# Low parts of float32r weight blocks: an accumulating DMA onto the negated high part in place of a VectorE subtraction

## The chip, the cores and the metric

The kernel runs on one core of a Trainium2 chip. The metric is device time in microseconds (us) of one execution; the lower, the better.

## The reference

A trunk of two decoder layers over 512 tokens of width 1024, all in float32. Each layer adds three things to the residual stream `x`, each of them after an RMSNorm:

```python
x = x + 0.5 * swiglu(rmsnorm(x, g1), w_gate1, w_up1, w_down1)   # 1024 -> 2816 -> 1024
p = rmsnorm(x, gm) @ w_in                                       # 1024 -> 3328, three mixers share it
x = x + concat(gmlp(p[:512]), shortconv(p[512:1280]), retention(p[1280:])) @ w_out
x = x + 0.5 * swiglu(rmsnorm(x, g2), w_gate2, w_up2, w_down2)
```

A final RMSNorm ends it. Nearly all of the arithmetic is in the products with the weights. A weight matrix is used once, so each of its 512 KB blocks is loaded from HBM once (in the kernel before) and used by 24 matmuls.

## The kernel before

**Products in parts.** TensorE takes float32r operands, which keep fewer bits than float32. So each operand `a` is split in a high part, `a` rounded to float32r, and a low part, what the rounding left over. A product is then three matmuls: high by high, high by low, low by high. `mm3` (L97) issues them as L99, L100 and L101. Activations are split once (`xh`, `xl`, and the two halves of `h`), weights block by block in `load` (L88): a DMA from SyncE brings 128x1024 float32 into `raw` (L92), ScalarE copies it with rounding into `whi` (L93), and VectorE subtracts `whi` from `raw` into `wlo` (L94). Some blocks hold 128x896. `load` is called 336 times; the first two blocks of the program are made in `start` (L185), in halves, with subtractions of their own (L210), which the change leaves alone.

**Buffers.** `raw` has 4 buffers, `whi` and `wlo` have 3 each (L83 to L85). A new block's `whi` and `wlo` can be written when the block three places before it has been used by its last matmul. Each engine works through its instructions in the order in which they were put in its queue; the tile framework orders them when the program is built, and puts the semaphore waits in.

**Stages.** In `gate_up` (L149) the weights are the stationary operand: block after block of 24 matmuls, first gate and then up of each of 22 feature tiles; behind each pair `finish` makes silu(gate) x up and splits it (VectorE L157, L160, L105, ScalarE L158, L104). In `ffn` (L217) the down product goes through pieces of 8, 7 and 7 blocks of 128 columns, 24, 21 and 21 matmuls (weights stationary, so the low weight part is first used by L101, the third matmul). `mixer` (L291) projects with 26 blocks; for values and gates (`project_tokens`) and in the last down product (`last_ffn`, L233) the tokens are the stationary operand and the low weight part is used by L100, the second matmul. Between them stand the small matmuls of retention and gMLP and the layer norms (`layernorm`, L495), whose reciprocal root is a GpSimd power (L510). GpSimd otherwise makes 1/rms in `norm_columns` (L134), masks a table (L302), and makes the final norm's factor (L285).

**End of the program.** The last three blocks of the last down product are all loaded ahead (L269), one into each buffer, and then used for one 128-token chunk and half of the features after the other, so that the final norm and the stores of a chunk run under the matmuls of the next.

Of the kernel before, what the change touches and what calls it, by code (L numbers as in the profile page):

```python
# [9 lines left out]
F32 = mybir.dt.float32  # L10
F32R = mybir.dt.float32r
AF = mybir.ActivationFunctionType
ALU = mybir.AluOpType
AX = mybir.AxisListType

P = 128
D = 1024
T = 512
DEPTH = 2
FF = 2816  # L20
KT = D // P
# [8 lines left out]

# Columns of the packed per-feature parameters.
G1, GM, G2 = 0, 8, 16
GV, GN, CW = 24, 26, 30
PER = 36
NPAR = DEPTH * PER

# Columns of the packed position constants.
C_COS, C_SIN, C_DEC, C_XI, C_ZETA = 0, 512, 1024, 1536, 2048
# [4 lines left out]
def trunk(ctx, tc, xt, w_gu1, w_dn1, w_in, w_out, w_gu2, w_dn2, w_last, par, con, wst, bst, gain, out):  # L43
    nc = tc.nc
# [19 lines left out]

# [1 line left out]
    x = [xpool.tile([P, T], F32, tag=f"x{k}", name=f"x{k}") for k in range(KT)]  # L66
    xh = [xpool.tile([P, T], F32R, tag=f"xh{k}", name=f"xh{k}") for k in range(KT)]
    xl = [xpool.tile([P, T], F32R, tag=f"xl{k}", name=f"xl{k}") for k in range(KT)]
    pcol = cpool.tile([P, NPAR], F32, name="pcol")
# [18 lines left out]
    def load(src):  # L88
        """One block of weights as two float32r parts whose sum it is."""
        n = src.shape[-1]  # L90
        raw, hi, lo = weight_tiles()
        nc.sync.dma_start(raw[:, :n], src)  # L92
        nc.scalar.copy(hi[:, :n], raw[:, :n])  # L93
        nc.vector.tensor_tensor(lo[:, :n], raw[:, :n], hi.bitcast(F32)[:, :n], ALU.subtract)  # L94
        return hi, lo

    def mm3(ps, ah, al, bh, bl, first, last):  # L97
        """ps += a.T @ b from their parts."""
        nc.tensor.matmul(ps, lhsT=ah, rhs=bh, start=first, stop=False)  # L99
        nc.tensor.matmul(ps, lhsT=ah, rhs=bl, start=False, stop=False)  # L100
        nc.tensor.matmul(ps, lhsT=al, rhs=bh, start=False, stop=last)  # L101
# [5 lines left out]
    state = {}  # L107
    warm_ps = bank("warm")

    def norm_part(k, gcol):  # L110
        """x[k] times its gain in two parts."""
        g = pcol[:, gcol + k : gcol + k + 1]
        nc.scalar.activation(xh[k], x[k], AF.Copy, scale=g)  # L113
        nc.vector.scalar_tensor_tensor(xl[k], x[k], g, xh[k].bitcast(F32), ALU.mult, ALU.subtract)  # L114
# [10 lines left out]
    def norm_columns():  # L125
        """1 / rms of each token, as columns [token, chunk]."""
        acc = state["acc"]
        ps = bank(uniq("pss"))
        for n in range(NCH):
            nc.tensor.matmul(ps[:, n : n + 1], lhsT=acc[:, n * P : (n + 1) * P], rhs=ones[:, 0:1], start=True, stop=True)  # L130
        ms = spool.tile([P, NCH], F32, tag="ms", name=uniq("ms"))
        nc.vector.tensor_scalar(ms, ps[:, :NCH], 1.0 / D, EPS, ALU.mult, ALU.add)
        rc = spool.tile([P, NCH], F32, tag="rc", name=uniq("rc"))
        nc.gpsimd.tensor_tensor(rc, ms, mhalf[:, :NCH], ALU.pow)  # L134
        state["rc"] = rc

    def norm_rows():
        """1 / rms of each token along the free axis, on every partition."""
        rc = state["rc"]
        pr = bank(uniq("psr"))  # L140
        dg = spool.tile([P, NCH, P], F32, tag="dg", name=uniq("dg"), bufs=1)
        for n in range(NCH):
            nc.vector.tensor_scalar(dg[:, n, :], ident, rc[:, n : n + 1], None, ALU.mult)
            nc.tensor.matmul(pr[:, n * P : (n + 1) * P], lhsT=ones, rhs=dg[:, n, :], start=True, stop=True)
        rr = spool.tile([P, T], F32, tag="rr", name=uniq("rr"))
        nc.scalar.copy(rr, pr)
        state["rr"] = rr

    def gate_up(l, w_gu, first=False):  # L149
        """h = silu(rms gate) * up, features on partitions."""  # L150
        hs = []
# [13 lines left out]
        for f in range(FT):  # L165
            ps = []
            if first and f == 0:
                ps = start(w_gu[l, 0, 0], w_gu[l, 1, 0])
            else:
                for j in range(2):  # L170
                    hi, lo = load(w_gu[l, j, f])
# [13 lines left out]
    def start(gate, up):  # L185
        """The first two blocks, with the splits of x between the first products."""
        for k in range(12):
            warm = warm_ps[:, (k % 4) * P : (k % 4 + 1) * P]
            nc.tensor.matmul(warm, lhsT=ones, rhs=ones, start=True, stop=True)
        ps = [bank(uniq("pgu")) for _ in range(2)]  # L190
        w = [weight_tiles() for _ in range(2)]
# [41 lines left out]
    def last_ffn(l, w_gu):  # L233
        """The last feed-forward, its second product and the final norm with tokens on partitions."""
        state.pop("rr", None)
        xtok = {}
        for f, hs in enumerate(gate_up(l, w_gu)):
            if f not in (4, 6):
                continue
            s = f // 6  # L240
# [50 lines left out]
    def mixer(l, after):  # L291
# [15 lines left out]
        def project(block, name):  # L307
            """One 128-feature block of the projection, features on partitions."""
            hi, lo = load(w_in[l, block])
            p = bank(uniq(name))  # L310
            for k in range(KT):
                c = slice(k * P, (k + 1) * P)
                mm3(p, hi[:, c], lo[:, c], xh[k], xl[k], k == 0, k == KT - 1)
            return p

        def project_tokens(block, name):
            """512 features of the projection (four blocks), tokens on partitions."""
            ps = [bank(uniq(name)) for _ in range(NCH)]
            for j in range(4):
                hi, lo = load(w_in[l, block + j])  # L320
                for n in range(NCH):
                    t = slice(n * P, (n + 1) * P)
                    for k in (2 * j, 2 * j + 1):
                        c = slice((k % 2) * T, (k % 2 + 1) * T)
                        mm3(ps[n], xh[k][:, t], xl[k][:, t], hi[:, c], lo[:, c], k == 0, k == KT - 1)
            return ps

        # Retention: rotated queries and keys.
        qk = [big(uniq("q")) for _ in range(2)] + [big(uniq("k")) for _ in range(2)]
        head = lambda w, h: qk[2 * w + h // 2][:, (h % 2) * T : (h % 2 + 1) * T]  # noqa: E731  # L330
        ahead = [project(0, "pqk")]
# [4 lines left out]
        for w in range(2):  # L336
            for h in range(HEADS):
# [10 lines left out]
                nc.vector.tensor_tensor(o, o, s, ALU.add)  # L348
        # Values, tokens on partitions.
        vt = [big(uniq("vt")) for _ in range(2)]  # L350
        tok = lambda tiles, n: tiles[n // 2][:, (n % 2) * T : (n % 2 + 1) * T]  # noqa: E731
        for n, p in enumerate(project_tokens(8, "pv")):
            nc.scalar.activation(tok(vt, n), p, AF.Copy, scale=rc[:, n : n + 1])
        # Queries for the state, keys with their decay to the chunk's end.
        qx = [big(uniq("qx")) for _ in range(2)]
# [18 lines left out]
        ys = [None] * KT  # L374
        # gMLP values, tokens on partitions.
        av = big(uniq("av"))
        hi, lo = load(w_in[l, 16])
        hi2, lo2 = load(w_in[l, 17])
        for n in range(NCH):
# [6 lines left out]
            nc.scalar.activation(av[:, n * 256 : (n + 1) * 256], p[:, :256], AF.Gelu_apprx_tanh, scale=rc[:, n : n + 1])  # L386
        # States ahead of chunks 1..3.
        st = [big(uniq("st")) for _ in range(2)]
# [19 lines left out]
        layernorm(av, av, NCH * AG, AH)  # L408
        # Gates.
        sg = [big(uniq("sg")) for _ in range(2)]  # L410
# [3 lines left out]
        for n in range(NCH):  # L414
# [11 lines left out]
            nc.vector.tensor_tensor(tok(yn, n), tok(yn, n), tok(sg, n), ALU.mult)  # L426
        # Short convolution.
        def conv(j):
# [5 lines left out]
            nc.vector.tensor_tensor(z[:, :T], z[:, :T], rr, ALU.mult)  # L434
            w = lambda i: pcol[:, base + CW + 2 * i + j : base + CW + 2 * i + j + 1]  # noqa: E731
            o = z[:, T:]
# [26 lines left out]
        conv(1)  # L463
        # Retention's outputs, features on partitions.
        for h in range(HEADS):
# [7 lines left out]
            ys[4 + h] = y  # L473
        # gMLP gates.
        for j in range(2):
# [19 lines left out]
    def layernorm(dst, src, groups, width):  # L495
        """(src - mean) / sqrt(var + eps) over groups of the free axis."""
        s3 = src.rearrange("p (g d) -> p g d", g=groups)
# [33 lines left out]
def _constants(np):  # L531
    """What depends on positions alone: rotary tables, decays."""
    half = P // 2
# [9 lines left out]
    scale = P**-0.5  # L543
# [8 lines left out]
def _layout(np, inp):  # L552
    """The inputs, each weight block as one contiguous run per partition."""
    f = lambda n: np.asarray(inp[n])  # noqa: E731
    arrays = {"xt": f("x").reshape(T, KT, P).transpose(2, 1, 0)}
# [7 lines left out]
    w = f("w_in")  # L563
    cols = lambda a, n: w[:, :, a : a + n]  # noqa: E731
    wide = lambda a, n, b: cols(a, n).reshape(DEPTH, b, KT // b, P, n).transpose(0, 1, 3, 2, 4).reshape(DEPTH, b, P, 1024)  # noqa: E731
    tall = lambda a, b: cols(a, b * P).reshape(DEPTH, KT, P, b, P).transpose(0, 3, 2, 1, 4).reshape(DEPTH, b, P, 1024)  # noqa: E731
    c0 = 1280
# [3 lines left out]
    arrays["w_out"] = f("w_out").reshape(DEPTH, KT, P, KT, P).transpose(0, 3, 2, 1, 4).reshape(DEPTH, KT, P, 1024)  # L571
    per = lambda a, n: a.reshape(n, P).T  # noqa: E731
    par = []
# [30 lines left out]
```

## Time and profile before

| | |
|---|---|
| time, median of 2 runs | 1877.43 us (1877.14 to 1877.72) |
| span of the profiled execution, first to last instruction | 1875.7 us |
| TensorE busy | 1865.6 us, 99% |
| VectorE busy | 839.3 us, 45% |
| ScalarE busy | 567.2 us, 30% |
| GpSimd busy | 27.4 us, 1% |
| read from HBM | 178.56 MB |

The profile is of one execution; its span leaves out what lies before the first and after the last instruction, here 1.7 us against the median of the timed runs. Engines are PE (TensorE), PEld (its weight loads), DVE (VectorE), ACT (ScalarE), POOL (GpSimd), SP (SyncE). Matmuls are pipelined: a row gives each 0.39 us, but one starts every 0.23 us, so it is starts that are compared. An issue of a DMA isn't counted as busy time.

### The profile page before, as it was taken

The page shows a single profiled execution, that of the slowest core. Times are in us where ns is not written, and L with a number is a line of the kernel's source. Part 1 is how long each engine was busy: PE and PEld are TensorE (multiplying, and loading weights), DVE is VectorE, ACT ScalarE, POOL GpSimd, SP SyncE. Part 2 cuts the span into 40 slices and gives each one's busy share as a digit, 9 for nine tenths or more (in the row PEclk, how much of TensorE's full clock was granted, in tenths as well). Part 3 has the DMA queues.
Part 4 walks back from the last instruction along what each step waited for, and adds up shares of the span by engine and source line. Part 5 has one row for each costly group of instructions (what it writes and reads, how often), then busy time and mean ns, then how long its engine had stood idle before and what let it go on. Part 6 is the DMA issues. An engine that isn't in the chain of part 4 may idle for free.

```text
span 1875.7 us, 20497 instructions
## 1 busy us (share of the span) xinstructions
PE 1865.6 (99%) x8560; PEld 1554.4 (83%) x8560; DVE 839.3 (45%) x1052; ACT 567.2 (30%) x713; POOL 27.4 (1%) x34
## 2 busy tenths in 40 slices
PE   9999999999999999999999999999999999999998
PEld 7888888888888888888888888888888888888886
DVE  5344334474664434433443444344647543444224
ACT  5223222223343322322232232222132433323212
POOL 0000000000000000000000000000000000000000
PEclk9999999999999999999999999999999999999999
DMA  5232333322222232233323223333322222332321
GB/s 203 102 97 94 99 93 93 114 94 75 84 90 97 95 101 91 99 93 95 106 90 102 91 100 96 94 93 108 102 79 79 91 92 89 100 100 92 113 94 64
DMA packets 52860, 181.98 MB, mean 97 GB/s; under 512 B 6048, under 2 KB 6560, under 8 KB 52640
## 3 DMA queue, kind: packets, MB, share of 16 engines
q1 hardware_dynamic: 52624, 180.64, 29.8%
q8 instruction: 67, 1.10, 0.2%
q14 instruction: 25, 0.20, 0.0%
q10 hardware_dynamic: 144, 0.04, 0.0%
HBM read 178.56 MB, written 2.10 MB: 96 GB/s over the span
## 4 chain that ended last, share of the span: by engine, by line
PE 98%; issue 0%; ACT 0%; DMA 0%; DVE 0%; SPq 0%; POOL 0%; POOLq 0%; ACTq 0%
PE pgu L99 17%; PE pgu L100 17%; PE pgu L101 17%; PE pdn L101 8%; PE pdn L100 8%; PE pdn L99 8%; PE pqk L99 2%; PE pqk L101 2%; PE pout L100 2%; PE pout L99 2%; PE pqk L100 2%; PE pout L101 2%; PE pv L101 1%; PE pg L99 1%; PE pg L101 1%; PE pg L100 1%
## 5 line engine op out<-in xcount | busy, mean ns | idle before, releaser
L93 ACT CAST whi<-raw 128x1024 fp32r<-128x1024 f32 (+1 forms) x336 | 348.6, 1038 | 1184.7 <-issue 365.1
L99 PE MATMUL pgu<-xh,whi 128*128 128x512 f32 x1408 | 548.6, 390 | 1.2 <-ACT xh L113 1.2
L100 PE MATMUL pgu<-xl,whi 128*128 128x512 f32 x1408 | 548.0, 389 | 0.7 <-DVE xl L114 0.6
L94 DVE TENSOR_TENSOR wlo<-raw,whi 128x1024 fp32r<-128x1024 f32 (+1 forms) x336 | 405.1, 1206 | 319.3 <-ACT whi L93 305.2
L101 PE MATMUL pgu<-xh,wlo 128*128 128x512 f32 x1408 | 548.0, 389 | 0.0
L99 PEld LDWEIGHTS pgu<-xh,whi 128*128 128x128 f32 x1408 | 264.2, 188 | 56.4 <-ACT xh L113 1.7
L100 PEld LDWEIGHTS pgu<-xl,whi 128*128 128x128 f32 x1408 | 264.3, 188 | 55.8 <-DVE xl L114 1.5
L101 PEld LDWEIGHTS pgu<-xh,wlo 128*128 128x128 f32 x1408 | 264.3, 188 | 55.5 <-DVE wlo L210 0.3
L99 PE MATMUL pdn<-h,whi 128*128 128x512 f32 x528 | 205.4, 389 | 0.0
L100 PE MATMUL pdn<-h,whi 128*128 128x512 f32 x528 | 205.4, 389 | 0.0
L101 PE MATMUL pdn<-h,wlo 128*128 128x512 f32 x528 | 205.4, 389 | 0.0
L160 DVE TENSOR_TENSOR b<-pgu,a 128x512 f32<-128x512 f32 x88 | 60.8, 692 | 280.2 <-PE pgu L101 277.8
L157 DVE TENSOR_TENSOR a<-pgu,rr 128x512 f32<-128x512 f32 x88 | 60.8, 691 | 220.0 <-PE pgu L101 220.0
L100 PEld LDWEIGHTS pdn<-h,whi 128*128 128x128 f32 x528 | 99.1, 188 | 20.6
L101 PEld LDWEIGHTS pdn<-h,wlo 128*128 128x128 f32 x528 | 99.1, 188 | 20.6
L99 PEld LDWEIGHTS pdn<-h,whi 128*128 128x128 f32 x528 | 99.1, 188 | 20.5
L100 PE MATMUL pdn<-wlo,h 128*128 128x512 f32 x176 | 68.6, 390 | 0.0
L101 PE MATMUL pdn<-whi,h 128*128 128x512 f32 x176 | 68.5, 389 | 0.0
L99 PE MATMUL pdn<-whi,h 128*128 128x512 f32 x176 | 68.4, 389 | 0.0
L105 DVE TENSOR_TENSOR h<-b,h 128x512 fp32r<-128x512 f32 x88 | 60.2, 685 | 2.1 <-ACT h L104 2.1
L104 ACT CAST h<-b 128x512 fp32r<-128x512 f32 x88 | 54.7, 622 | 2.7 <-DVE b L160 2.5
L158 ACT ACTIVATE a<-a 128x512 f32<-128x512 f32 x88 | 55.0, 626 | 1.3 <-DVE a L157 1.3
(179 smaller groups left out, 1641.9 us busy)
## 6 DMA issues: line engine op xcount, KB each, us to landing
raw<-in_w_gu SPq DMA_DIRECT2D x174, 512.0 KB, 3.3
raw<-in_w_in SPq DMA_DIRECT2D x52, 512.0 KB, 3.3
raw<-in_w_dn SPq DMA_DIRECT2D x48, 448.0 KB, 3.3
raw<-in_w_dn SPq DMA_DIRECT2D x24, 512.0 KB, 3.5
raw<-in_w_last SPq DMA_DIRECT2D x22, 512.0 KB, 3.3
raw<-in_w_out SPq DMA_DIRECT2D x16, 512.0 KB, 3.3
x<-in_xt SPq DMA_DIRECT2D x8, 256.0 KB, 6.6
out<-o SPq DMA_DIRECT2D x8, 256.0 KB, 2.2
```

Source lines behind the costliest of these rows:

```text
L93: nc.scalar.copy(hi[:, :n], raw[:, :n])
L94: nc.vector.tensor_tensor(lo[:, :n], raw[:, :n], hi.bitcast(F32)[:, :n], ALU.subtract)
L99: nc.tensor.matmul(ps, lhsT=ah, rhs=bh, start=first, stop=False)
L100: nc.tensor.matmul(ps, lhsT=ah, rhs=bl, start=False, stop=False)
L101: nc.tensor.matmul(ps, lhsT=al, rhs=bh, start=False, stop=last)
L104: nc.scalar.copy(h, src)
L105: nc.vector.tensor_tensor(lo, src, h.bitcast(F32), ALU.subtract)
L157: nc.vector.tensor_tensor(a, ps[0], rr, ALU.mult)
L158: nc.scalar.activation(a, a, AF.Silu)
L160: nc.vector.tensor_tensor(b, ps[1], a, ALU.mult)
```

## The change

In `load`, the low part is no longer subtracted on VectorE. ScalarE writes the rounded weights a second time, negated, into `wlo`; then GpSimd issues a DMA that reads the same weight block from HBM again and adds it to what stands in `wlo`. The result is again the weights less their rounded part.

```diff
         raw, hi, lo = weight_tiles()
         nc.sync.dma_start(raw[:, :n], src)
         nc.scalar.copy(hi[:, :n], raw[:, :n])
-        nc.vector.tensor_tensor(lo[:, :n], raw[:, :n], hi.bitcast(F32)[:, :n], ALU.subtract)
+        nc.scalar.activation(lo[:, :n], raw[:, :n], AF.Copy, scale=-1.0)
+        nc.gpsimd.dma_start(lo[:, :n], src, accum_op=ALU.add)
         return hi, lo
```

The rest of the diff removes comments and docstrings. Because `load` grew by a line, line numbers behind it are one higher in the kernel after: the high copy is L93 in both, the negated copy L94, the accumulating DMA L95, and the three matmuls of `mm3` are L100, L101 and L102.

The order in which the engines take their instructions moves at three places that the prediction speaks of. The first is TensorE behind the two blocks of `start`. Before, it takes the third block of the program (`whi_243`, `wlo_244`) straight through:

```order
L101 MATMUL pgu_129<-xh_91,wlo_135 128x512
L99 MATMUL pgu_248<-xh_84,whi_243 128x512
L100 MATMUL pgu_248<-xl_92,whi_243 128x512
L101 MATMUL pgu_248<-xh_84,wlo_244 128x512
L99 MATMUL pgu_248<-xh_85,whi_243 128x512
```

After:

```order
L102 MATMUL pgu_129<-xh_91,wlo_135 128x512
L100 MATMUL pgu_249<-xh_84,whi_243 128x512
L101 MATMUL pgu_249<-xl_92,whi_243 128x512
L131 MATMUL pss_274<-ones,acc_219 128x1 x4
L100 MATMUL pgu_290<-xh_84,whi_284 128x512
L101 MATMUL pgu_290<-xl_92,whi_284 128x512
L145 MATMUL psr_315<-dg_316,ones 128x128 x4
L102 MATMUL pgu_249<-xh_84,wlo_244 128x512
```

Two matmuls of the next block and both small products of the norm now stand ahead of the first use of the low part `wlo_244`.

The second place is TensorE in the last three blocks of the program (high and low parts 12329/12330, 12335/12336 and 12341/12342 before). Before, the first use of the last block's low part is the twelfth matmul there:

```order
L99 MATMUL pdn_11750<-whi_12329,h_11597 128x512
L100 MATMUL pdn_11750<-wlo_12330,h_11597 128x512
L101 MATMUL pdn_11750<-whi_12329,h_11597 128x512
L99 MATMUL pdn_11750<-whi_12335,h_11667 128x512
L100 MATMUL pdn_11750<-wlo_12336,h_11667 128x512
L101 MATMUL pdn_11750<-whi_12335,h_11667 128x512
L99 MATMUL pdn_11750<-whi_12341,h_11737 128x512
L99 MATMUL pdn_11751<-whi_12329,h_11597 128x512
L100 MATMUL pdn_11751<-wlo_12330,h_11597 128x512
L101 MATMUL pdn_11751<-whi_12329,h_11597 128x512
L99 MATMUL pdn_11751<-whi_12335,h_11667 128x512
L100 MATMUL pdn_11750<-wlo_12342,h_11737 128x512
```

After (the parts are 12662/12663, 12669/12670 and 12676/12677), nine matmuls stand ahead of this piece in those three blocks; its last row is the first use of the last low part, the 21st matmul:

```order
L100 MATMUL pdn_12064<-whi_12676,h_12051 128x512
L100 MATMUL pdn_12065<-whi_12669,h_11979 128x512
L101 MATMUL pdn_12065<-wlo_12670,h_11979 128x512
L102 MATMUL pdn_12065<-whi_12669,h_11979 128x512
L100 MATMUL pdn_12065<-whi_12676,h_12051 128x512
L100 MATMUL pdn_12066<-whi_12662,h_11907 128x512
L101 MATMUL pdn_12066<-wlo_12663,h_11907 128x512
L102 MATMUL pdn_12066<-whi_12662,h_11907 128x512
L100 MATMUL pdn_12066<-whi_12669,h_11979 128x512
L101 MATMUL pdn_12066<-wlo_12670,h_11979 128x512
L102 MATMUL pdn_12066<-whi_12669,h_11979 128x512
L101 MATMUL pdn_12064<-wlo_12677,h_12051 128x512
```

The first use of the last block's low part moves back by nine matmuls.

The third place is GpSimd in the first layer's retention, where it makes the reciprocal roots of the four layer norms (`rs`). Before, they follow each other:

```order
L510 TENSOR_TENSOR rs_3145<-var_3142,mhalf 128x16
L510 TENSOR_TENSOR rs_3294<-var_3291,mhalf 128x4
L510 TENSOR_TENSOR rs_3316<-var_3313,mhalf 128x4
L510 TENSOR_TENSOR rs_3338<-var_3335,mhalf 128x4
L510 TENSOR_TENSOR rs_3360<-var_3357,mhalf 128x4
```

After:

```order
L95 DMA wlo_3522<-in_w_in 128x1024
L511 TENSOR_TENSOR rs_3378<-var_3375,mhalf 128x4
L511 TENSOR_TENSOR rs_3400<-var_3397,mhalf 128x4
L511 TENSOR_TENSOR rs_3422<-var_3419,mhalf 128x4
L511 TENSOR_TENSOR rs_3444<-var_3441,mhalf 128x4
L95 DMA wlo_3580<-in_w_in 128x1024
```

The DMA for the low part of the second convolution's first block (`wlo_3580`) now stands behind the four powers in the same queue.

## Rows read from the trace of the kernel before

**Rows 1.** The page: busy time of the engines, and the chain that ended last.

```profile
PE 1865.6 (99%) x8560; PEld 1554.4 (83%) x8560; DVE 839.3 (45%) x1052; ACT 567.2 (30%) x713; POOL 27.4 (1%) x34
...
PE 98%; issue 0%; ACT 0%; DMA 0%; DVE 0%; SPq 0%; POOL 0%; POOLq 0%; ACTq 0%
```

**Rows 2.** TensorE's waits: who was waited for, us in total, times, longest.

```profile
PE pgu L99 <- ACT xh L113: 1.2, 1, 1.2
PE warm L189 <- DVE deps L251: 1.1, 1, 1.1
PE pgu L100 <- DVE xl L114: 0.6, 1, 0.6
```

**Rows 3.** Groups by shape on ScalarE and VectorE: xcount | busy us, mean ns | idle.

```profile
L93 ACT CAST whi<-raw 128x1024 fp32r<-128x1024 f32 x288 | 303.2, 1053 | 1003.6 <-issue 365.1 <-PE pgu L100 333.0 <-PE pdn L101 82.8
L158 ACT ACTIVATE a<-a 128x512 f32<-128x512 f32 x88 | 55.0, 626 | 1.3 <-DVE a L157 1.3
L104 ACT CAST h<-b 128x512 fp32r<-128x512 f32 x88 | 54.7, 622 | 2.7 <-DVE b L160 2.5
L93 ACT CAST whi<-raw 128x896 fp32r<-128x896 f32 x48 | 45.4, 946 | 181.0 <-PE pdn L100 153.8 <-PE pgu L100 23.2 <-PE pdn L101 4.0
...
L94 DVE TENSOR_TENSOR wlo<-raw,whi 128x1024 fp32r<-128x1024 f32 x288 | 352.7, 1225 | 244.6 <-ACT whi L93 233.0
...
L94 DVE TENSOR_TENSOR wlo<-raw,whi 128x896 fp32r<-128x896 f32 x48 | 52.5, 1093 | 74.7 <-ACT whi L93 72.3
```

**Rows 4.** Timeline, one gate/up block: start us, us, engine, line, what, [idle <- releaser].

```profile
108.85 0.39 PE L101 MATMUL pgu<-xh,wlo 128*128 128x512 f32 x1
109.08 0.39 PE L99 MATMUL pgu<-xh,whi 128*128 128x512 f32 x1
109.09 1.06 ACT L93 CAST whi<-raw 128x1024 fp32r<-128x1024 f32 x1 [3.86 <-issue]
110.07 0.62 ACT L104 CAST h<-b 128x512 fp32r<-128x512 f32 x1
110.18 1.23 DVE L94 TENSOR_TENSOR wlo<-raw,whi 128x1024 fp32r<-128x1024 f32 x1
119.96 0.39 PE L99 MATMUL pgu<-xh,whi 128*128 128x512 f32 x1
120.41 0.39 PE L101 MATMUL pgu<-xh,wlo 128*128 128x512 f32 x1
```

**Rows 5.** Timeline, the 24-matmul block of a down product.

```profile
285.89 1.05 ACT L93 CAST whi<-raw 128x1024 fp32r<-128x1024 f32 x1 [1.49 <-issue]
295.85 0.39 PE L101 MATMUL pdn<-h,wlo 128*128 128x512 f32 x1
```

**Rows 6.** DMA: a queue's share of the 16 engines; issues, KB, us to landing.

```profile
q1 hardware_dynamic: 52624, 180.64, 29.8%
...
raw<-in_w_gu SPq DMA_DIRECT2D x174, 512.0 KB, 3.3
...
ct<-in_con SPq DMA_DIRECT2D x1, 1026.0 KB, 7.1
```

**Rows 7.** Timeline, the first block behind `start`.

```profile
16.44 1.03 ACT L93 CAST whi<-raw 128x1024 fp32r<-128x1024 f32 x1
20.16 0.39 PE L99 MATMUL pgu<-xh,whi 128*128 128x512 f32 x1
25.60 0.95 PE L130 MATMUL pss<-ones,acc 128*128 128x1 f32 x8
26.41 0.49 PE L99 MATMUL pgu<-xh,whi 128*128 128x512 f32 x1
```

**Rows 8.** Timeline, the last block's high part and the matmuls of the end.

```profile
1851.89 0.39 PE L99 MATMUL pdn<-whi,h 128*128 128x512 f32 x1
1852.09 1.05 ACT L93 CAST whi<-raw 128x1024 fp32r<-128x1024 f32 x1 [4.38 <-PE pdn L101]
```

**Rows 9.** Timeline, the last layer norm of retention and the block behind.

```profile
495.00 1.21 DVE L94 TENSOR_TENSOR wlo<-raw,whi 128x1024 fp32r<-128x1024 f32 x1
496.44 1.01 POOL L510 TENSOR_TENSOR rs<-var,mhalf 128x4 f32<-128x4 f32 x1 [3.88 <-DVE var L508]
503.99 0.40 PE L101 MATMUL pcg<-xh,wlo 128*128 128x512 f32 x1
```

## The prediction

> **What bounds the kernel now.** I read the page first, then TensorE's waits, then the groups by shape, then single blocks in the timeline, and the DMA view last. The page says that TensorE is busy for 1865.6 of 1875.7 us and holds 98% of the chain that ended last [rows 1]. Its own waits come to 2.9 us, all of them in the first microseconds [rows 2]. So no engine that feeds it is late, and the 10.1 us in which it isn't busy are a ceiling on any gain: 0.5%, under the 2% (37.5 us) that a measurement of this kernel can tell from no change. What VectorE is spared can't show as time. The question is only whether the new way of making the low part still comes in time.
>
> How much time it has is read from one gate/up block. The last matmul of the block three places before starts at 108.85; the high copy starts 0.24 us later, at 109.09, since it waits for that buffer; the low part is written at 110.18 for 1.23, so it is ready at 111.41; the block's first matmul starts at 119.96 and the first that reads the low part at 120.41 [rows 4]. The low part lies ready for 9.0 us. From 109.08 to 119.96 there are two blocks, 10.88 us, so a block takes 5.44 us, 0.227 us for each of its 24 matmuls. The kernel runs like this nearly everywhere, because three buffers always leave two blocks of time.
>
> **What goes.** 336 subtractions on VectorE, 352.7 + 52.5 = 405.2 us [rows 3]. None was on the path, so this is worth nothing, but for the layer norms below.
>
> **ScalarE.** It gets 336 negated copies. The same rounding copy of the same tile takes 1053 ns, or 946 for the narrow ones, and an activation takes what a copy takes (626 against 622 ns at 128x512) [rows 3]. So 303.2 + 45.4 = 348.6 us come to the 567.2 it has [rows 1], 916 us or 49% of the span. In a block it then does two copies and one instruction of `finish`, 1.06 + 1.05 + 0.62 = 2.7 of 5.44 us [rows 4]. The instruction of `finish` comes 1.05 us later; it has spare PSUM banks behind it, so I cost this at nothing. If that cover were gone it would be 1.05 us a block, 350 us. The `raw` buffer is freed by the negated copy where it was freed by the subtraction; four buffers leave the next load of SyncE's queue some 4 x 5.44 - 2 = 19.8 us for the 3.3 that it takes [rows 6]. SyncE's order doesn't change. Nothing.
>
> **The accumulating DMA.** This is new and no row of before has one, nor any DMA of GpSimd. From the start of the high copy the chain is now two ScalarE copies, 2.11 us, then the DMA from GpSimd's issue to landing, L. It may take up to 120.41 - 109.09 - 2.11 = 9.2 us before TensorE waits [rows 4]. In every third block of a down product, with only two blocks of 21 matmuls ahead of it, it may take 295.85 - 285.89 - 2.10 = 7.9 us [rows 5]. Bounds for L: it can't be under the 3.3 us of a plain load of the same 512 KB, because it moves these bytes and reads the tile besides. The nearest row for twice the bytes is the load of 1026 KB, 7.1 us [rows 6]. At the far end each of three passes (read HBM, read the tile, write it), beside the plain load of another block that is released at the same moment, is paid like a load: four times 512 KB, twice that row, 14.2 us. I take 7.1: an accumulate has two streams of 512 KB to read, which is what the row is nearest to. With 7.1 every steady block is covered, by 2.1 us in gate/up and by 0.8 in the tightest down block, and costs nothing. If the cover goes, each buffer is late by L - 9.2 once in three blocks, so the price is 336/3 = 112 times (L - 9.2).
>
> The Trainium skill, DMA: Bandwidth & Descriptors, section "Anatomy of one DMA — SWDGE (gpsimd) path", gives a DMA issued from GpSimd about 2.0 us plus its bytes at 436 GB/s. By it, as an estimate with 1 MB to read, L would be 4.4 us, and the whole sum below 1879. No row of before shows such a DMA.
>
> **Where there is no lead of two blocks.** Three places.
>
> At the start, the high copy runs at 16.44 for 1.03 [rows 7], the negated copy until 18.6, so the low part lands at 25.7. TensorE gets there at 20.16 [rows 7]. In the new order it has four matmuls (0.9 us) and the two small norm products (0.8 us for the first, from 25.60 to 26.41 [rows 7], the second taken alike) to do first, until 22.7. It then waits 3.0 us. The following low parts have more time.
>
> At the end, the last block's copies wait for the buffer until 1852.09; with the negated copy first, the DMA is issued at 1853.14 and lands at 1860.2. TensorE begins these three blocks at 1851.89 [rows 8] and, in the new order, has 20 matmuls, 4.5 us, until it needs it, at 1856.4. It waits 3.8 us, and the final norms and stores come as much later.
>
> In retention, GpSimd's queue puts one block's DMA behind four powers that wait for VectorE. Before, the last of them starts at 496.44 for 1.01, and that block's low part is needed at 503.99 [rows 9]: 497.45 + 7.1 = 504.6 would be 0.6 us late, in each of two layers. But a subtraction that is gone, 1.21 us at 495.00 [rows 9], stood right ahead of what the power waits for; so I take zero (bounds 0 and 1.2 us for both). The powers themselves stand behind DMAs whose ScalarE copies were released a block earlier; they are not late.
>
> **The sum.** 1875.7 + 3.0 + 3.8 = 1882.5 of span; with the 1.7 us between this span and the median of the runs, 1884.2. I forecast 1884 us: no change that can be told.
>
> **Rivals.**
>
> A. *The 16 DMA engines fill up (slower).* The loads take 29.8% of their time now [rows 6]. The accumulates carry the same bytes again. If one costs r times a plain load, the share becomes 29.8 x (1 + r): 89% at r = 2, full at r = 2.36, and 119% at r = 3, which makes the span 1875.7 x 1.19 = 2236 us. It decides from r = 2.36 on. For it: the margin is small, and adding may be slower than copying. Against: at r = 2 it fits.
>
> The Trainium skill, Collectives: The Full Stack, section "The bandwidth ceiling: the fold count and why AG ≠ RS ≠ AR", holds that the add in a DMA costs no cycles of its own, but two reads instead of one, and so half the rate. By it r is 2 and the share stays at 89%, short of full; no row of before shows it.
>
> B. *Latency (slower).* The engines have room, but L is over 9.2 us: GpSimd takes long to write the descriptors, or adding to a tile in place goes row after row. From L = 9.5 on it is over 2%: 112 x 0.3 = 34 us on top of 5 us more at start and end. At L = 11 it is 112 x 1.8 = 202 on top of 1884 + 8, some 2094 us. For it: nothing in before bounds GpSimd's part. Against: 2.1 us of reserve.
>
> C. *Like a plain load.* L is 3.3 to 4.5. Then the start waits for 18.6 + 4.5 = 23.1 against 22.7, the end for 1857.6 against 1856.4, and the time is 1877 to 1879.
>
> D. *A gain.* At most the 10.1 us; over 2% is out of reach.
>
> **Chances.** My case 0.40, C 0.20, A 0.18, B 0.21, D over 2% 0.01. So within 2% is 0.60, slower 0.39, faster 0.01; the likeliest two alone span 1874 to 1895. To leave out no more than 2 in 10 the range must take in B up to L = 11.5, about 2150, and leaves A.
>
> **What would show it.** Right: 336 DMAs of GpSimd that land after about 7 us; TensorE at 1865 us busy with waits for `wlo` only at the start (3 us) and in the last three blocks (4 us); ScalarE near 916 us, VectorE near 434; a DMA share below 90%. Wrong: rows in TensorE's waits in which L101 or L102 wait for the DMA of `wlo` a hundred times and more, and blocks further apart than 5.44 us. If the DMA share is then near full it is A, if it is well below it is B. A GpSimd that is busy for most of a block would put B on the descriptors.

## The result and the profile after

The changed kernel took 1894.92 us (median of two runs, 1894.03 to 1895.82) against 1877.43 us: a ratio of 1.0095, with a 95% interval of 1.0076 to 1.0114. It is slower by about 1%, inside the 2% that were called no change. The profiled execution took 1895.82 us, its span 1894.1 against 1875.7, so the span grew by 18.4 us where the prediction had added 6.8.

The page of the kernel after, to be laid beside [rows 1] and [rows 6]: busy time, queues, and the chain that ended last.

```profile
PE 1871.8 (99%) x8560; PEld 1555.0 (82%) x8560; DVE 450.4 (24%) x716; ACT 873.4 (46%) x1049; POOL 317.4 (17%) x370
...
q0 software_dynamic: 48384, 173.04, 52.6%
q1 hardware_dynamic: 52624, 180.64, 32.7%
...
PE 54%; issue 35%; POOL 7%; DMA 3%; ACT 1%; POOLq 0%; DVE 0%; SPq 0%; ACTq 0%
```

VectorE's 405 us are gone from it, ScalarE has its second copy, and queue q0, the accumulating DMA, keeps the 16 engines busier than the plain loads of q1 do. The chain reads as if TensorE had lost half its part. It has not: it is busy for 1871.8 us. The chain steps off TensorE at a wait of a fraction of a microsecond and then follows the DMA back through the queues that issued it, past time in which TensorE was working. Where the engine that bounds the time has short waits, its idle time and its waits say more than the chain does. Idle time is 1894.1 - 1871.8 = 22.3 us where it was 10.1; that is 12.2 of the 18.4 us, and the other 6.2 are in longer busy time: the matmuls at the lower clock (below), and the part of each short gap that a matmul's record covers.

TensorE's waits after, in the columns of [rows 2]:

```profile
PE pgu L102 <- DMA wlo<-in_w_gu: 6.1, 2, 5.7
PE pav L101 <- DMA wlo<-in_w_in: 2.1, 2, 1.7
PE pdn L101 <- DMA wlo<-in_w_last: 1.7, 2, 1.3
...
PE psr L145 <- DVE dg L144: 1.1, 1, 1.1
PE pdn L102 <- DMA wlo<-in_w_dn: 0.9, 4, 0.3
```

All the new waits but one are for a low part. Of 336 accumulates TensorE waits for eleven by this view (the one small wait left out of the lines above included).

The groups that answer to [rows 3], wide and narrow tiles together, and the DMA view that answers to [rows 6] (issues, KB, median us to landing):

```profile
L94 ACT ACTIVATE wlo<-raw 128x1024 fp32r<-128x1024 f32 (+1 forms) x336 | 348.5, 1037 | 115.6 <-PE pdn L101 64.4 <-PE pg L101 28.0 <-PE pv L101 21.4
L93 ACT CAST whi<-raw 128x1024 fp32r<-128x1024 f32 (+1 forms) x336 | 347.7, 1035 | 841.6 <-issue 805.9 <-PE pout L101 21.3 <-PE pgu L101 14.1
```

```profile
raw<-in_w_gu SPq DMA_DIRECT2D x174, 512.0 KB, 5.9
wlo<-in_w_gu POOLq DMA_DIRECT2D x174, 512.0 KB, 7.7
```

Over all 336 accumulates, from the view of their line (from GpSimd's issue):

```profile
DMA to landing us min/median/max: 5.2/7.6/11.4
```

So the term L, taken at 7.1, is 7.6 in the median. But it has a tail up to 11.4, and the plain load beside it went from 3.3 us to 5.9.

**Where the 18.4 us went.** Both kernels issue 8560 matmuls, so the start of each one after less the start of the one at the same place in the order before is the lag of TensorE at that point. It is 9.2 us by 50 us into the span. From there it stays level, but for nine single gaps between 320 and 1384 us (0.16 to 1.85 us each, 5.2 in all, the remaining 1.4 in smaller ones), and is 15.8 at 1390. The last three blocks add 2.0 and the last store 0.6.

*The start.* The timeline of the first block behind `start`, to be laid beside [rows 7]:

```profile
17.91 1.05 ACT L94 ACTIVATE wlo<-raw 128x1024 fp32r<-128x1024 f32 x1
19.28 1.03 POOL L95 DMA_DIRECT2D wlo<-in_w_gu  x1 [17.90 <-ACT wlo L94]
19.37 0.42 SPq L524 DMA_DIRECT2D ct<-in_con  x1
...
22.30 0.40 PE L101 MATMUL pgu<-xl,whi 128*128 128x512 f32 x1
23.82 1.25 PE L145 MATMUL psr<-dg,ones 128*128 128x128 f32 x8 [1.13 <-DVE dg L144]
30.77 0.79 PE L102 MATMUL pgu<-xh,wlo 128*128 128x512 f32 x1 [5.69 <-DMA wlo<-in_w_gu]
31.36 0.63 PE L100 MATMUL pgu<-xh,whi 128*128 128x512 f32 x1
```

And the windows of the same stretch, with a long steady one at the end. The columns are start and end, us, busy time of PE, PEld, DVE, ACT and POOL (instructions), the granted clock, the DMA engines' share, GB/s:

```profile
22.00:26.00 4.00, 1.95 (x12) 1.29 (x11) 1.33 (x6) 1.72 (x3) 1.93 (x2) 1.00 0.91 271
26.00:30.00 4.00, 0.00 (x0) 0.00 (x0) 1.11 (x2) 3.18 (x4) 0.86 (x1) 0.60 1.06 274
30.00:34.00 4.00, 3.23 (x8) 2.58 (x9) 0.69 (x1) 0.00 (x0) 0.00 (x0) 0.55 1.04 271
34.00:38.00 4.00, 4.00 (x19) 3.33 (x18) 0.63 (x1) 0.81 (x1) 0.00 (x0) 1.00 0.45 92
600.00:800.00 200.00, 200.00 (x887) 165.77 (x886) 39.36 (x57) 95.59 (x114) 32.03 (x37) 1.00 0.89 191
```

The first accumulate is issued at 19.28 and lands 11.4 us later, the longest of the landings above. Until 34 us the DMA engines have no room (share 0.91, 1.06, 1.04): the preloaded blocks, the table `ct` issued 0.09 us later, and the first accumulates are all under way. TensorE waits 5.69 us. Behind the wait the granted clock is 0.60 and 0.55: of the two levels, 2.4 and 1.2 GHz, it is at the lower one for most of these eight microseconds. Seven steps between matmuls, from 30.77 to 33.77, come 0.43 us apart on average instead of 0.227, which costs 3.00 - 7 x 0.227 = 1.4 us. The third part is the 1.13 us in front of the small products with `dg`, which used to stand behind matmuls of the block and are now reached with nothing else to do. These are 8.2 of the 9.2 us.

*The short gaps.* Five of the nine are in down products; the largest single one, 1.85 us, is ahead of the gMLP values of the second layer. The accumulate for them was issued at 1374.80, its block was wanted 7.0 us later, and it took 8.8; the two accumulates before it took 9.4 and 10.6. A down product, to be laid beside [rows 5]:

```profile
355.76 1.05 ACT L93 CAST whi<-raw 128x1024 fp32r<-128x1024 f32 x1 [2.51 <-issue]
356.71 1.05 ACT L94 ACTIVATE wlo<-raw 128x1024 fp32r<-128x1024 f32 x1
358.06 0.86 POOL L95 DMA_DIRECT2D wlo<-in_w_dn  x1 [4.79 <-ACT wlo L94]
...
365.49 0.39 PE L101 MATMUL pdn<-h,whi 128*128 128x512 f32 x1
366.07 0.50 PE L102 MATMUL pdn<-h,wlo 128*128 128x512 f32 x1 [0.19 <-DMA wlo<-in_w_dn]
```

The negated copy ends at 357.76, GpSimd issues 0.30 us later, and the low part is there 8.0 us after that, at 366.07. It was wanted 0.227 us behind the matmul at 365.49, at 365.72. That is 7.96 us after the copy, the prediction's 7.9, against 8.3: 0.35 us late. The trace's own 0.19 is less than the gap between the starts, since the ends of matmuls are modelled. The gaps are therefore read from starts.

*The end*, for which [rows 8] stood, is the wait of `pdn` L101 for `in_w_last` above: 1.7 us in two waits.

### The profile page after: what moved, and what is told of

The parts are those of the page before. It is cut to its first block, busy times and chain, and to the rows that moved or that the text cites. A ratio compares the mean times of both kernels' runs of the same rounds, so it can differ in the third digit from the quotient of the medians.

```text
span 1894.1 us, 21333 instructions
## 1 busy us (share of the span) xinstructions
PE 1871.8 (99%) x8560; PEld 1555.0 (82%) x8560; DVE 450.4 (24%) x716; ACT 873.4 (46%) x1049; POOL 317.4 (17%) x370
## 2 busy tenths in 40 slices
DMA packets 101252, 355.08 MB, mean 187 GB/s; under 512 B 11424, under 2 KB 11936, under 8 KB 101024
## 3 DMA queue, kind: packets, MB, share of 16 engines
q0 software_dynamic: 48384, 173.04, 52.6%
q1 hardware_dynamic: 52624, 180.64, 32.7%
## 4 chain that ended last, share of the span: by engine, by line
PE 54%; issue 35%; POOL 7%; DMA 3%; ACT 1%; POOLq 0%; DVE 0%; SPq 0%; ACTq 0%
PE pgu L100 8%; PE pgu L102 8%; PE pgu L101 8%; POOL wlo L95 6%; PE pdn L102 5%; PE pdn L101 5%; PE pdn L100 5%; PE pout L101 2%; PE pout L102 2%; PE pout L100 2%; DMA wlo<-in_w_dn 1%; DMA wlo<-in_w_in 1%; PE pg L102 1%; PE pg L101 1%; PE pg L100 1%
## 5 line engine op out<-in xcount | busy, mean ns | idle before, releaser
L93 ACT CAST whi<-raw 128x1024 fp32r<-128x1024 f32 (+1 forms) x336 | 347.7, 1035 | 841.6 <-issue 805.9
L102 PE MATMUL pgu<-xh,wlo 128*128 128x512 f32 x1408 | 548.6, 390 | 6.1 <-DMA wlo<-in_w_gu 6.1
L100 PE MATMUL pgu<-xh,whi 128*128 128x512 f32 x1408 | 549.2, 390 | 0.8 <-ACT xh L114 0.8
L101 PE MATMUL pgu<-xl,whi 128*128 128x512 f32 x1408 | 548.6, 390 | 0.5 <-DVE xl L115 0.4
L94 ACT ACTIVATE wlo<-raw 128x1024 fp32r<-128x1024 f32 (+1 forms) x336 | 348.5, 1037 | 115.6 <-PE pdn L101 64.4
L102 PEld LDWEIGHTS pgu<-xh,wlo 128*128 128x128 f32 x1408 | 264.7, 188 | 61.8 <-DMA wlo<-in_w_gu 6.7
L100 PEld LDWEIGHTS pgu<-xh,whi 128*128 128x128 f32 x1408 | 264.5, 188 | 56.7 <-ACT xh L114 2.0
L101 PEld LDWEIGHTS pgu<-xl,whi 128*128 128x128 f32 x1408 | 264.6, 188 | 56.4 <-DVE xl L115 1.8
L95 POOL DMA_DIRECT2D wlo<-in_w_gu x174 | 151.1, 869 | 804.4 <-ACT wlo L94 792.5
L102 PE MATMUL pdn<-h,wlo 128*128 128x512 f32 x528 | 206.2, 390 | 0.9 <-DMA wlo<-in_w_dn 0.9
L100 PE MATMUL pdn<-h,whi 128*128 128x512 f32 x528 | 205.5, 389 | 0.0
L101 PE MATMUL pdn<-h,whi 128*128 128x512 f32 x528 | 205.5, 389 | 0.0
L102 PEld LDWEIGHTS pdn<-h,wlo 128*128 128x128 f32 x528 | 99.1, 188 | 23.9 <-DMA wlo<-in_w_dn 3.5
L101 PEld LDWEIGHTS pdn<-h,whi 128*128 128x128 f32 x528 | 99.1, 188 | 20.7
L100 PEld LDWEIGHTS pdn<-h,whi 128*128 128x128 f32 x528 | 99.1, 188 | 20.4
L95 POOL DMA_DIRECT2D wlo<-in_w_dn x72 | 62.3, 865 | 302.2 <-ACT wlo L94 296.5
L230 DVE SCALAR_TENSOR_TENSOR y<-pdn,rr 128x512 f32<-128x512 f32 x24 | 16.6, 692 | 278.9 <-PE pdn L102 278.9
L95 POOL DMA_DIRECT2D wlo<-in_w_in x52 | 45.7, 879 | 215.5 <-ACT wlo L94 215.4
L101 PE MATMUL pdn<-wlo,h 128*128 128x512 f32 x176 | 68.7, 390 | 1.7 <-DMA wlo<-in_w_last 1.7
```

The lines of the kernel that those rows point to most:

```text
L94: nc.scalar.activation(lo[:, :n], raw[:, :n], AF.Copy, scale=-1.0)
L95: nc.gpsimd.dma_start(lo[:, :n], src, accum_op=ALU.add)
L230: nc.vector.scalar_tensor_tensor(y, p, 0.5, rr, ALU.mult, ALU.mult)
```

## The experiments

The theory was that the loss has two parts and no third: the first accumulate, which finds the DMA engines full and starves TensorE, and blocks whose cover is just shorter than the slow accumulates. The rivals were a slow drain in every block (the doubled copies on ScalarE, GpSimd's part, the traffic as such), and a loss that comes from the table `ct` alone. Ratios are to runs of the kernel before on the same chip, with 95% intervals; where one run was made, only its time is given.

**1. The first three blocks subtract on VectorE as before.**

```diff
     def load(src):
...
         nc.scalar.copy(hi[:, :n], raw[:, :n])
+        count[0] += 1
+        if count[0] <= 3:
+            nc.vector.tensor_tensor(lo[:, :n], raw[:, :n], hi.bitcast(F32)[:, :n], ALU.subtract)
+            return hi, lo
         nc.scalar.activation(lo[:, :n], raw[:, :n], AF.Copy, scale=-1.0)
```

> The changed kernel, but the first three blocks behind start get their low part by the VectorE subtraction again; the other 333 by the accumulating DMA. Theory 1 (the time is lost at a few places without a lead of two blocks, most of it at the start, where TensorE idles 6 us for the first accumulate and then runs some microseconds at half clock): TensorE no longer waits before 50 us, the granted clock stays at full, and the span falls by 8 to 9 us, to about 1885.5. Theory 2 (the accumulates slow the whole program a little, by the doubled DMA traffic or by ScalarE's second copy, and the start only shows part of it): it falls by less than 3 us.

Measured: 1887.13 us (four runs), ratio 1.0060 (1.0043 to 1.0077), span 1883.6. TensorE does not wait at the start. Its window there:

```profile
26.00:30.00 4.00, 4.00 (x19) 3.29 (x18) 0.87 (x4) 0.52 (x1) 1.86 (x2) 1.00 0.68 230
```

Without the wait the granted clock is 1.00 from 26 to 30 us, where it was 0.60. The lag at 50 us is -1.1 us instead of +9.2, so the start is worth 10.3 us, and the span fell by 10.5. With the subtractions TensorE's order at the start is that of the kernel before again, so the wait for `dg` goes too: the run gives back the start as a whole. It is 1.1 us ahead of the kernel before because the wait of 1.2 us for `xh` [rows 2] did not come up in it. The fall is that of one execution, the fastest of four (1885.38 to 1890.75 us), against the slower of two; the medians are 7.8 us apart. What comes behind is about as before: from -1.1 to 5.1 us by 1304 us, again in single gaps, nine of the twelve in down products, and to 5.4 by 1390, so 6.5 us where it was 6.6.

**2. The table is loaded later.** A copy of one column from the input makes `ct`'s load wait; it is overwritten by that load.

```diff
         if l == 0:
+            nc.vector.tensor_copy(ct[:, 0:1], x[0][:, 0:1])
             nc.sync.dma_start(ct, con)
```

> The changed kernel, but the 1026 KB table of position constants, which is loaded at 19.4 us, just when the first accumulate is issued, is held back until the first down product (its load waits for a one-column copy of x). Theory 1a (the first accumulate takes 11.4 us and not 7.6 because the 16 DMA engines are full of other loads then, this table among them): the first accumulate lands 2 to 3 us earlier, the wait of 5.7 us falls to about 3, and the span by 3 to 4 us. Theory 1b (the first accumulate is long for a reason of its own, its place as the first DMA of its queue): it lands as late as before and the span changes by less than 1 us.

Measured: 1893.17 us (four runs), ratio 1.0090 (1.0075 to 1.0105), span 1890.4. The first accumulate took 7.6 us where it had taken 11.4, so it was not long for being the first of its queue. It landed 5.0 us earlier, 1.1 of them because it was also issued earlier (18.15, not 19.28), before the table could matter. The wait of 5.7 us at the start became 1.7, and the lag there 5.2 instead of 9.2. The granted clock still fell, since the wait for `dg` and the 1.7 us still leave TensorE idle. The table took its crowd along. Its load now goes at 272.90, beside an accumulate issued at 272.78, which took 10.5 us, the longest of this run:

```profile
DMA to landing us min/median/max: 5.0/7.6/10.5
```

The down product that needed it started 1.6 us late. Of the 4.0 us won at the start 3.7 reach the end of the span in the profiled execution, but it is the fastest of four; the medians differ by 1.75 us with overlapping intervals. So the table is a part of the crowd at the start, less than half of the loss there, and what moving it is worth in time is not settled.

**3. The same DMA without the addition.** The low part is then a plain copy of the block; the products with it are of other numbers.

```diff
-        nc.gpsimd.dma_start(lo[:, :n], src, accum_op=ALU.add)
+        nc.gpsimd.dma_start(lo[:, :n], src)
```

> The changed kernel with the same DMA from GpSimd, but plain: it overwrites the low part with the weights instead of adding to it, so the low parts hold the weights themselves. It measures what the addition costs. If an accumulate is two reads at the price of one each: 4096-byte packets of GpSimd's queue take about 160 ns instead of 328, the queue's share of the engines falls from 52.6% to about 28%, and landing from 7.7 to about 5 us. If the queue of GpSimd itself is slow, the packets stay over 250 ns and landing over 6.5 us. The time is 1880 to 1888 either way.

Measured: 1883.55 us in one run, span 1881.9, with one wait for a low part, 2.6 us at the start. The queue, and the landings of line L95:

```profile
q0 software_dynamic: 48384, 173.04, 26.0%
```

```profile
DMA to landing us min/median/max: 3.4/4.5/8.3
```

Same packets, same bytes, half the engine time. Share times 16 engines times span over packets: 0.526 x 16 x 1894.1 / 48384 = 0.329 us for a packet that adds, 0.260 x 16 x 1881.9 / 48384 = 0.162 for one that copies, a factor of 2.03. (Both are means over all packets of the queue, of which one in nine is small: under 512 B there are 11424 packets on the page after and 6048 on that before.) The addition costs 3.1 us of landing, 4.5 to 7.6, and with them all the gaps behind the start but one of 0.3 us in the last three blocks. The start still has 5.3 us of lag, so the loss there is not the addition alone. The Trainium skill, Collectives: The Full Stack, section "The bandwidth ceiling: the fold count and why AG ≠ RS ≠ AR", says of the add in a reduce-scatter around a ring of cores that it costs a second source read and no cycles, and so about half the rate. No run here counts the reads; the factor of 2.03 agrees with it.

**4. Four buffers for the low part, three for the raw block** (four of each don't fit beside the rest).

```diff
-        raw = wpool.tile([P, 1024], F32, tag="raw", name=uniq("raw"), bufs=4)
+        raw = wpool.tile([P, 1024], F32, tag="raw", name=uniq("raw"), bufs=3)
...
-        lo = wpool.tile([P, 1024], F32R, tag="wlo", name=uniq("wlo"))
+        lo = wpool.tile([P, 1024], F32R, tag="wlo", name=uniq("wlo"), bufs=4)
```

> The changed kernel with four buffers of low parts instead of three; raw blocks have three instead of four to make room (they had 20 us of lead for a load of 6). An accumulate may then take some 5.4 us more before TensorE waits. Theory 1: the waits behind the start (down products, gMLP values, the last three blocks; 5 to 6 us together, with what their order costs) go, the wait at the start stays: 4 to 9 us less than the changed kernel. Theory 2 (a slowdown spread over all blocks, not waits): under 2 us less.

Measured: 1884.18 us (five runs), ratio 1.0036 (1.0023 to 1.0049), span 1882.4. The medians are 10.7 us apart, more than the 4 to 9 expected, because the wait at the start shrank too, from 5.7 to 1.9 us. No wait for a low part is left behind the start; the lag is 6.0 us, all of it from the start. Two things changed in the blocks behind it. A steady block, after and then in this run, whose DMA view follows (the row of 16.65 us is four loads in one, so its start is that of the first):

```profile
700.58 16.65 SPq L92 DMA_DIRECT2D raw<-in_w_gu  x4
700.84 0.86 POOL L95 DMA_DIRECT2D wlo<-in_w_gu  x1 [4.56 <-ACT wlo L94]
703.98 1.05 ACT L93 CAST whi<-raw 128x1024 fp32r<-128x1024 f32 x1 [2.92 <-issue]
704.94 1.05 ACT L94 ACTIVATE wlo<-raw 128x1024 fp32r<-128x1024 f32 x1
```

```profile
703.68 1.05 ACT L93 CAST whi<-raw 128x1024 fp32r<-128x1024 f32 x1 [2.91 <-PE pgu L101]
704.63 1.06 ACT L94 ACTIVATE wlo<-raw 128x1024 fp32r<-128x1024 f32 x1
704.75 0.33 SPq L92 DMA_DIRECT2D raw<-in_w_gu  x1
705.98 0.86 POOL L95 DMA_DIRECT2D wlo<-in_w_gu  x1 [4.58 <-ACT wlo L94]
```

```profile
raw<-in_w_gu SPq DMA_DIRECT2D x174, 512.0 KB, 3.4
wlo<-in_w_gu POOLq DMA_DIRECT2D x174, 512.0 KB, 5.8
```

The first is the lead. In the kernel after, the two ScalarE rows belong to one block, high part first. In this run the program's order is turned round: a block's negated copy, for which there is a buffer more, stands ahead of its high copy. The row at 704.63 is therefore the negated copy of the block behind the one whose high copy stands at 703.68. From GpSimd's issue to the first matmul that reads the low part there are now 14.4 us in the median, where there were 9.0: one block more.

The second is the plain load. It is issued when the high copy ends, as the raw block's negated copy was made a block earlier, and so 1.23 us ahead of the accumulate where it was 0.26. It lands in 3.4 us, as in [rows 6], not 5.9; the accumulate lands in 5.8, not 7.7. Either change covers the 0.35 us by which the down product above was late, and this run does not separate them. Runs 3 and 7, with the old lead of 9.0 us and landings of 4.5 and 5.1 us, have no wait for a low part between the start and the last three blocks either.

At the start this run shows the price of the clock again. TensorE waits there for 1.1 and 1.9 us, less than in the kernel after, and the granted clock is at the lower level from 22 us on:

```profile
22.00:26.00 4.00, 2.08 (x8) 1.78 (x8) 1.30 (x4) 1.82 (x3) 0.56 (x2) 0.50 1.05 274
```

Fourteen such steps from 26.04 to 32.16 take 6.12 - 14 x 0.227 = 2.9 us more than at full speed, twice the 1.4 us behind the longer wait.

**5. Both, 1 and 4 together** (the two diffs above).

> Both mends together: the first three blocks behind start by subtraction, and four buffers of low parts (three of raw) for the accumulates of the other 333. If the changed kernel's loss is the wait at the start plus the waits of a lead that is too short, and nothing else, the span is that of the kernel before within 1.5 us (1874 to 1877), the time 1876 to 1879. If the doubled DMA traffic or ScalarE's second copy costs something by itself, 3 us or more over the kernel before remain.

Measured: 1877.44 us (ten runs) against 1876.94, ratio 1.0003 (0.9994 to 1.0013), span 1875.1. Its page and all of TensorE's waits:

```profile
PE 1865.3 (99%) x8560; PEld 1554.4 (83%) x8560; DVE 454.0 (24%) x719; ACT 871.2 (46%) x1046; POOL 313.7 (17%) x367
```

```profile
PE warm L196 <- DVE deps L258: 1.1, 1, 1.1
PE pgu L107 <- DVE xl L121: 0.4, 1, 0.4
PE pgu L106 <- ACT whi L216: 0.4, 1, 0.4
```

The two parts make up the whole loss. 333 accumulates and as many negated copies are still there, the DMA engines are nearly as busy (54.0 + 28.6 = 82.6%), and nothing is lost to them: no drain in every block. It also shows that VectorE's 385 us less buy nothing.

**6. Two buffers for the low part**, which takes one block of lead away. A loop that holds three blocks at its end has to hold two.

```diff
-        lo = wpool.tile([P, 1024], F32R, tag="wlo", name=uniq("wlo"))
+        lo = wpool.tile([P, 1024], F32R, tag="wlo", name=uniq("wlo"), bufs=2)
...
-        tail = FT - 3
+        tail = FT - 2
```

> The changed kernel with two buffers of low parts instead of three (and two blocks instead of three left for the interleaved end, so that they fit). It tests the price of a lead that is missing. The lead falls by one block, 5.44 us, from 9.2 to 3.8 us; with an accumulate that lands 7.6 us after its issue and 0.3 us between ScalarE and GpSimd, each buffer is late by 4.1 us once in two blocks: 336/2 x 4.1 = 690 us more, a time near 2580 us (2450 to 2700). If instead the DMA engines or GpSimd were what limits, fewer buffers would change little: under 2000 us.

Measured: 2808.89 us in one run, span 2807.2: a miss, 109 us above the range. Its page, its largest wait, and a window:

```profile
PE 2183.0 (78%) x8560; PEld 1727.9 (62%) x8560; DVE 449.8 (16%) x716; ACT 872.3 (31%) x1049; POOL 316.8 (11%) x370
```

```profile
PE pgu L102 <- DMA wlo<-in_w_gu: 326.6, 103, 5.8
```

```profile
100.00:300.00 200.00, 152.77 (x574) 119.92 (x572) 24.91 (x36) 60.48 (x72) 20.70 (x24) 0.89 0.56 124
```

All its waits for low parts come to 608 us, 597 more than after, where some 690 were forecast; by them alone it would take some 2490 us. The rest is in busy time: 2183.0 - 1871.8 = 311 us for the same matmuls, at a mean granted clock of 0.887 (0.89 in this window). 597 + 311 are 908 of the 913 us between the spans. The price of a late buffer was right in kind; that an idle TensorE comes back at the lower clock was left out, as it was in the prediction.

**7. No plain loads.** One raw block is loaded once, and all high parts and negated copies are made from it. The high parts are then not those of the block in turn, though the sum of high and low parts still is, since the accumulate adds the true weights to the negated high part; the expectation says this otherwise.

```diff
-        raw, hi, lo = weight_tiles()
-        nc.sync.dma_start(raw[:, :n], src)
+        _, hi, lo = weight_tiles(False)
+        raw = one_raw
+        if not loaded:
+            loaded.append(1)
+            nc.sync.dma_start(raw, src)
```

> The changed kernel without the plain loads of load: one raw block is loaded once, and all high parts and negated copies are made from it, so the products are of other numbers; the 336 accumulates stay as they are. Issue to landing of an accumulate alone: if the plain load released at the same moment is what lengthens it from the two reads' own time (plain 4.5 us plus 16 x 8 packets' worth of doubled time, 1.3 us, so 5.8) to 7.6, it lands in 5.5 to 6.2 us, and no wait is left behind the start. If it keeps 7 us or more, the rest is GpSimd's and the addition's own. Share of the queue as before, about 52%.

Measured: 1881.28 us in one run, span 1879.3. Landings of its accumulates (the plain queue has 1.2% of the engines left, where it had 32.7%):

```profile
DMA to landing us min/median/max: 4.9/5.1/7.5
```

Alone, an accumulate of 512 KB lands in 5.1 us, less than the 5.5 to 6.2 expected; 2.5 of the 7.6 us come from the plain load released at the same moment. One wait for a low part is left, 1.5 us in the last three blocks, which have no lead of two blocks; none was expected.

**8. No accumulating DMA.** The low part is the negated high part; what the DMA adds is left out.

```diff
         nc.scalar.activation(lo[:, :n], raw[:, :n], AF.Copy, scale=-1.0)
-        nc.gpsimd.dma_start(lo[:, :n], src, accum_op=ALU.add)
         return hi, lo
```

> The changed kernel without the accumulating DMA: the low part stays the negated high part. ScalarE does its 336 second copies, VectorE is spared the subtractions, DMA traffic is that of the kernel before. If ScalarE's copies are covered and VectorE's relief is worth nothing: 1876 to 1880 us, TensorE waits of under 4 us. If ScalarE's copies cost: over 1885. If the relief of VectorE is worth something: under 1874.

Measured: 1877.24 us in one run, span 1875.1, TensorE waiting 1.5 us in all.

```profile
PE 1865.9 (100%) x8560; PEld 1555.5 (83%) x8560; DVE 450.3 (24%) x716; ACT 873.5 (47%) x1049; POOL 24.9 (1%) x34
```

The doubled copies on ScalarE cost nothing that one run can show, and the relief of VectorE is worth nothing (1877.24 against 1876.94 for the kernel before). All of the loss is in the DMA.

## Why the prediction was right, and where its size was off

The forecast, no change that can be told, holds: 1894.92 us is 0.93% above before, with nearly every accumulate behind TensorE's work. Its 1884 us were 10.9 too low, and the span grew by 18.4 us where it had added 6.8. That 1894.9 is still inside its likeliest two cases, 1874 to 1895, by 0.1 us, is luck; that the loss is small, since all but eleven accumulates are covered, is not.

- *336 subtractions worth nothing:* right (run 8). VectorE has 450 us where 434 were expected.
- *ScalarE covered:* right (run 8). The two copies take 347.7 + 348.5 us, each as the 348.6 forecast. The busy time is 873 and not 916 mainly because back-to-back instructions overlap in the records: the copy of 1.05 us at 355.76 is followed by one at 356.71, so 0.10 us is counted once, 336 times, which makes 34 of the 43 us.
- *L = 7.1:* 7.6 in the median, a fair size by a poor reason. The row it leaned on was a load of twice the bytes; in fact 5.1 is the accumulate and 2.5 its collision with the plain load (run 7), which the prediction had only in its far end. The estimate of 4.4 us that the Trainium skill gave (DMA: Bandwidth & Descriptors, "Anatomy of one DMA — SWDGE (gpsimd) path") is nearer to the 5.1 us that it takes alone; in the kernel the measurement decides, 7.6.
- *"It then waits 3.0 us" at the start:* this is the step that failed. The wait was 5.69 us. L was taken as anywhere else, while the preloads and the table held every DMA engine, and it was 11.4: the low part landed at 30.7 where 25.7 was forecast. The norm products were reckoned as work that fills time, while they had a wait of 1.13 us of their own: TensorE came to them at 22.7, but to the first use of the low part only at 25.1, where 22.7 was forecast. That made the wait for the low part shorter and not the loss. And a TensorE that had stood idle was reckoned to come back at full speed. 9.2 us in place of 3.0, and run 1 gives them back.
- *"costs nothing" for the steady and the tightest down blocks:* the second miss. The allowance of 7.9 us was right to a tenth (the stall at 366.07), but the hand-over from ScalarE's copy to GpSimd's issue, 0.3 us, was not in it, and one value of L was put against it as if every DMA took it. The margin of 0.8 was less than the spread. The nine gaps of the middle, in down, projection, gate/up and gMLP blocks, come to 5.2 us and the lag there to 6.6. Run 3 takes them away by a shorter L, run 4 by a longer lead and a shorter L together.
- *End, 3.8:* 2.0 and 0.6 us. Its waits are 1.7 us.
- *Retention, 0:* right; no product of the convolution behind the layer norms waits.
- *Rivals.* A: the accumulates take 52.6% where the loads before took 29.8, so r is 1.8 against these (2.03 against a plain DMA of the same queue, run 3), near the step with r = 2; the share is 52.6 + 32.7 = 85.3%, below 90 and not full, and of the stretches read at the start only those up to 34 us are. B: the median L is 7.6, well under 9.2. Behind the start single ones are longer, 10.6 at most in the kernel after and 9.2 in run 1; the four over 9.2 in the kernel after had leads of 9.8 to 11.0 and were not waited for. GpSimd takes 0.87 us for an issue and is busy 17%. C fell with run 3, which shows what it would have been, 4.5 us. D: no run's median is below that of the kernel before.
- *Two slips in the working change nothing.* The high copy at 109.09 waits for the last matmul that reads the high part, which is the one ahead of the row at 108.85 (in [rows 3] L100 is named, not L101). And 1875.7 x 1.19 is 2232; the 2236 goes with 119.2%.

## What to carry to other kernels

When work goes from a compute engine to a DMA, the buffer lead is the budget, and the transfer's slow tail, with the hand-over in front of it, has to fit in it, not its median. Look first at the places that have no steady lead (the first blocks, the last, blocks of fewer matmuls), and read the DMA share of just those microseconds. One buffer more for the part that the DMA completes can lengthen the lead by a block (run 4). And where the engine that was relieved is not the bound, as VectorE here at 45%, the move had nothing to win: the best version of it that was run, number 5, takes the time of the kernel before.

## What was not expected of the hardware

- How far apart a plain load and an accumulate are issued changes the landing more than the engines' mean share does. The accumulate lands in 5.8 us when it goes 1.23 us behind the load (run 4, with the 16 engines at 82.7%), in 7.7 when it goes 0.26 behind (after, 85.3%), and in 7.8 at 0.26 in run 6, where the engines are at 57.4%. The plain load's own landing is less clear: 3.4 and 4.5 us (runs 4 and 5) at 1.23, 5.9 and 3.9 (after and run 6) at 0.26.
- What the lower granted clock adds to a wait is not in proportion to the wait. At the start it added 1.4 us behind a wait of 5.7 (the clock was 0.60 in 26 to 30 us), but 2.9 us in run 4 behind waits of 1.1 and 1.9. In run 6, with waits of up to 5.8 us throughout, it added 311 us to 608.
